# Weight sums for a seven-product last down projection, moved from the first FFN to the second up projection

## The chip, the cores and the metric

One core of a Trainium2 chip runs the whole program. The metric is the device time of one launch in microseconds (us). The engines are named as in the profile: PE (TensorE matmul), PEld (its weight load), DVE (VectorE), ACT (ScalarE), POOL (GpSimd), SP (SyncE). POOL, SP and ACT also issue DMAs.

## The reference

A decoder trunk of two layers on 512 tokens of width 1024, all in float32. Each layer has a token mixer and then a gated MLP (FFN); one RMSNorm ends it. What matters here is the FFN:

```python
D_FF, CONV_WIDTH, DEPTH = 2816, 3, 2
def conv_ffn(h, w_up, conv_w, conv_b, w_down):
    u = h @ w_up                       # (512, 1024) @ (1024, 5632)
    up = jnp.pad(u, ((0, 0), (CONV_WIDTH - 1, 0), (0, 0)))
    c = conv_b
    for j in range(CONV_WIDTH):
        c = c + conv_w[j] * up[:, j:j + S]
    gate, val = jnp.split(c, 2, axis=-1)
    return (jax.nn.silu(gate) * val) @ w_down      # (512, 2816) @ (2816, 1024)
...
for l in range(DEPTH):
    ...
    x = x + conv_ffn(rmsnorm(x, norm2_g[l]), ffn_w_up[l], ffn_conv_w[l], ffn_conv_b[l], ffn_w_down[l])
return rmsnorm(x, final_g)
```

## The kernel before, in words

**Matmuls.** Every float32 operand is split into a rounded high part and a low remainder, and a product is made of three matmuls (`mm3`, L153): high by low, high by high, low by high. The high part is a copy by ACT (L140 for weights, L149 for activations), the low part a subtraction by DVE (L141, L150).

**Weights.** `unit` (L95) hands out 128 x 512 pieces of weights by a plan that a first dry pass has noted. SP loads a piece into one of three buffers `wr` (L127), ACT and DVE split it into `sh`/`sl` or `wh`/`wl` (`part`, L131), up to `AHEAD` pieces before PE needs it (three in the FFN). A buffer is free for the next load once DVE has made the low part.

**The order of the work.** A tile scheduler orders each engine's instructions, by its own times for them; what is passed through `keep_in_program_order` keeps the order in which the program emits it. Each engine's list is executed in order, and an instruction that waits holds up what stands behind it on its engine.

**The up projection** (`ffn_up`, L1072) makes 22 pairs of output tiles, a gate tile and a value tile of 128 channels by 512 tokens. An output tile takes 24 matmuls. DVE then multiplies it by the row norm (`fu`, L1100), ACT makes the first tap of the convolution with the bias (`cv`, L1102), DVE adds two more taps (L1103, L1104); after both tiles of a pair ACT makes the silu and DVE the product (`fth`, L1109). In the second layer every other iteration up to the 16th also transposes a block of the residual through DRAM (`turned`, L226: a DVE transpose and five DMAs on POOL).

**The last down projection** (`last`, L1154) is not made as 8 products of blocks, but by a Strassen-like scheme with 7: the two halves of the tokens and neighbouring blocks of 128 channels are combined, in activations and in weights. `halves` (L1121) combines the activations of a pair of iterations on DVE: sums and differences of 256 columns each (L1130, L1131, L1132, L1134), of which some are split at once and some go to DRAM (`ab`, `s4`) by POOL. L1134 writes its difference into the tile `b`, whose old content POOL has just sent to DRAM (L1129). The combined weights are four tiles of 128 x 512 for each of the 11 groups of two blocks. `last` uses weight kinds 7, 5, 6, 4 of each group first (six matmuls for each, from `tsum`, DRAM tiles named `ts`), then the plain ones.

**The weight sums** (`presum`, L238). For each of the 11 groups POOL loads four tiles `pre` from `wdt` (L254), DVE makes four sums in place (L243 to L246, `b3 -= b1`, `b1 -= b0`, `b0 += b3`, `b2 -= b0`), and POOL stores them into `ts` (L249). This doesn't depend on any activation. A table, `PRE`, puts groups 0 to 3 at iterations 2, 4, 6 and 8 of the first layer's up projection, in 16 tiles of the FFN's large pool, and groups 4 to 10 at output tiles 0 to 6 of the first layer's down projection, in tiles of the general pool `u`; each call makes the sums of the group loaded by the call before. The scheduler is free to place them.

Of the kernel before, what the change touches and what calls it, by code (L numbers as in the profile page):

```python
# [15 lines left out]
L = 2  # L16
# [3 lines left out]
NFF = 22  # L20
# [3 lines left out]
FIRST = (12, 4, 0, 8)  # L24
FILL = (36, 2, 1)
KEPT = 6
PRE = {(0, "f", 2): 0, (0, "f", 4): 1, (0, "f", 6): 2, (0, "f", 8): 3, (0, "d", 0): 4, (0, "d", 1): 5, (0, "d", 2): 6, (0, "d", 3): 7,
       (0, "d", 4): 8, (0, "d", 5): 9, (0, "d", 6): 10}
SEQ = "0 H 0 S 0 U S U S 0 S 0 0 S 2 2 Y 0 0 2 1 2 1 2 1 2 1 2 1 2 1 1 1"
NRAW = 3  # L30
AHEAD = {None: 2, "p": 4, "r": 3, "f": 3, "u": 5, "q": 4}
DEEP = 6
EXP_HALF = math.exp(-0.5)
# [19 lines left out]
class Emit:  # L53
    def __init__(self, ctx, tc, a, plan=None):

        self.plan, self.used = plan, []
        self.raws, self.parts, self.nraw, self.npart = [], [], 0, 0
        self.pool, self.fp, self.pin, self.keep, self.turn = None, None, False, False, 4
        self.tc, self.nc, self.a = tc, tc.nc, a
        tp = lambda n, b, **k: ctx.enter_context(tc.tile_pool(name=n, bufs=b, **k))  # L60
        self.cp = tp("cp", 1)
        self.wp = tp("wp", 2)
        self.up = tp("up", NU)
        self.rg = tp("rg", NR)
        self.sp = tp("sp", 2)
        self.pa = tp("pa", 4, space=bass.MemoryType.PSUM)
        self.ps = tp("ps", 4, space=bass.MemoryType.PSUM)
        self.dp = tp("dp", 1, space=bass.MemoryType.DRAM)
        self.cnt = 0
# [52 lines left out]
    def load(self, u):  # L122
        name, l, i, c0, n, _ = u
        raw = self.u(n="wr") if u[5] == "q" and self.nraw % 2 else self.wp.tile([128, 512], F32, name=self.nm("wr"), tag="wr", bufs=NRAW)
        src = self.tsum[i] if name == "tsum" else self.a[name][l, i]
        with self.tc.high_priority():
            self.kept(self.nc.sync.dma_start(raw[:, :n], src[:, c0:c0 + n]))  # L127
        self.raws.append(raw)
        self.nraw += 1
# [105 lines left out]
        q.dma_start(d, t)  # L235
        return d

    def presum(self, l, stage, m):  # L238

        if self.pre:  # L240
            q, b = self.pre.pop()
            V = self.nc.vector
            V.tensor_tensor(b[3], b[3], b[1], op=SUB)  # L243
            V.tensor_tensor(b[1], b[1], b[0], op=SUB)
            V.tensor_tensor(b[0], b[0], b[3], op=ADD)
            V.tensor_tensor(b[2], b[2], b[0], op=SUB)  # L246
            for p, t in zip((7, 5, 6, 4), (b[3], b[1], b[0], b[2])):
                self.tsum[q, p] = self.dp.tile([128, 512], F32, name=self.nm("ts"))
                self.nc.gpsimd.dma_start(self.tsum[q, p], t)  # L249
        q = PRE.get((l, stage, m))  # L250
        if q is not None:
            b = self.fpre.pop(0) if stage == "f" else [self.u(n="pre") for _ in range(4)]
            for i, t in enumerate(b):
                self.nc.gpsimd.dma_start(t, self.a["wdt"][0, 2 * q + i // 2][:, i % 2 * 512:i % 2 * 512 + 512])  # L254
            self.pre.append((q, b))

    def norm_new(self):
        return {"z": [], "acc": None}
# [77 lines left out]
    def run(self):  # L336
        nc, tc, a, V = self.nc, self.tc, self.a, self.nc.vector
        self.con = self.cp.tile([128, NCC], F32, name="con")
        self.pre, self.tsum = [], {}
        self.rst = self.cp.tile([128, 512], F32, name="rst")  # L340
        self.bonesR = self.cp.tile([128, 128], F32R, name="bonesR")
        self.ones = self.cp.tile([128, 128], F32R, name="ones")
        V.memset(self.rst, 1.0)
        wu = self.acc()
        for i in range(5):
            nc.tensor.matmul(wu[:, 0:256], self.rst[:, 0:128], self.rst[:, 256:512], start=True, stop=True)
        self.pc = self.sp.tile([128, 64], F32, name="g1", tag="g1", bufs=1)
        st = self.norm_new()
        xs = [self.u(n="x") for _ in range(8)]
        self.keep = True  # L350
        with tc.high_priority():
            tc.keep_in_program_order(nc.scalar.dma_start(self.pc[:, 0:8], a["pcols"][0][:, PC["n1"]:PC["n1"] + 8]))
            for j in range(8):
                tc.keep_in_program_order((nc.scalar if j in (1, 3) else nc.sync).dma_start(xs[j], a["xT"][:, j, :]))
                if self.plan and j in (0, 1, 2):
                    self.load(self.plan[self.nraw])
        tc.keep_in_program_order(nc.scalar.copy(self.small((128, 1), "ms"), self.rst[:, 0:1]))
        tc.keep_in_program_order(nc.scalar.copy(self.ones, self.rst[:, 0:128]))
        for step in "z0 w z1 w z2 w z3 s0 s1 w z4 s2 z5 s3 w c z6 s4 w z7 s5 s6 s7 w w".split():
            if step == "w":  # L360
                if self.plan:
                    if self.nraw == self.npart:
                        self.load(self.plan[self.nraw])
                    self.part(self.plan[self.npart])
            elif step == "c":
                g1 = self.pc
                self.load_pc(0)
                tc.keep_in_program_order(nc.scalar.dma_start(self.con, a["con"]))
                self.pc, g1 = g1, self.pc
            elif step[0] == "z":  # L370
                self.norm_z(st, xs[int(step[1])], "n1")
            else:
                self.norm_sq(st, xs[int(step[1])])
        self.keep, self.pc = False, g1
        xd = [a["xT"][:, j, :] for j in range(8)]
        for l in range(L):
            mg = self.mixer(l, st)
            st = self.norm_new()
            x = self.wout(l, mg, xd, st)
            st["sq"] = self.split(st["acc"])  # L380
            act = self.ffn_up(l, st, x if l == L - 1 else None)
            if l == L - 1:
                self.last(act)
            else:
                st = self.norm_new()
                x, xd = self.ffn_down(l, act, x, st)
                st["sq"] = self.split(st["acc"])
            self.rp.__exit__(None, None, None)
            self.fp = None
# [682 lines left out]
    def ffn_up(self, l, st, x):  # L1072
# [7 lines left out]

        act, pair = [], []
        first = self.firstF(l, (78, 79, 80), st, 3)
        if l == 0:
            self.fpre = [[self.f(n="pre") for _ in range(4)] for _ in range(4)]
        for i in range(NFF):
            if l == 0 and i % 2 == 0 and 2 <= i <= 10:
                self.presum(l, "f", i)
            if x and i % 2 == 1 and i < 17:
                o = self.r(n="xt")
                self.turned(o, self.r(n="xT"), x[i // 2], nc.gpsimd)  # L1090
# [3 lines left out]
            for j in (i, NFF + i):  # L1094
                ps = first.pop(0) if first else self.colF(l, 78 + 2 * i + (j >= NFF))
                if pair:
                    act.append(self.halves(*pair, i // 2 - 1, at))
                    pair = []
                u = self.u(n="fu")
                V.tensor_tensor(u, ps, self.rsF, op=MUL)  # L1100
                t = self.u(n="cv")
                A.activation(t, u, AF.Identity, scale=self.p("cw2", j), bias=self.p("cb", j))  # L1102
                V.scalar_tensor_tensor(t[:, 1:], u[:, :511], self.p("cw1", j), t[:, 1:], op0=MUL, op1=ADD)  # L1103
                V.scalar_tensor_tensor(t[:, 2:], u[:, :510], self.p("cw0", j), t[:, 2:], op0=MUL, op1=ADD)  # L1104
                cs.append(t)
            g, v = cs
            th = self.u(n="fth")
            A.activation(th, g, AF.Silu)
# [12 lines left out]
    def halves(self, a, b, q, at):  # L1121
# [9 lines left out]
        V.tensor_tensor(s[:, h[1]], s[:, h[0]], a[:, h[0]], op=SUB)  # L1131
        V.tensor_tensor(d[:, h[0]], b[:, h[0]], s[:, h[1]], op=SUB)  # L1132
        P.dma_start(self.s4[:, h[q % 2]], d[:, h[0]])
        V.tensor_tensor(b[:, h[0]], a[:, h[0]], a[:, h[1]], op=SUB)  # L1134
        return self.split(s, at), self.split(b, at), ab, self.s4

    def ffn_down(self, l, act, x, st):
        nc, V = self.nc, self.nc.vector
# [2 lines left out]
        for m in range(8):  # L1141
# [5 lines left out]
            d = self.dp.tile([128, 512], F32, name=self.nm("xd"))  # L1147
            nc.gpsimd.dma_start(d, x[m])
            xd.append(d)
            self.presum(l, "d", m)  # L1150
        return x, xd


    def last(self, act):  # L1154
# [7 lines left out]

        def unit(p, q):
            if p > 3:
                return self.unit("tsum", 0, (q, p), 0)
            return self.unit("wdt", 0, 2 * q + (p > 1), 512 * (p == 3))

        def prod(ps, x, at, r, w, first, end, **kw):
# [27 lines left out]
        def half(ps):  # L1196
            t = self.u(n="e")
            po(A.activation(t, ps, AF.Copy, scale=0.5))
            return t
# [25 lines left out]
        for q in range(Q):  # L1225
            self.keep = q > 1
            s, t = act[q][:2]
            for p in (7, 5, 6, 4) if q < Q - 1 else (6, 7, 5, 4):
# [6 lines left out]
                if q == Q - 1 and p in (6, 7):  # L1235
                    for r in range(2):
                        (e1 if p == 6 else f0).append(half(pss[p][r]))
            if q == 1:
                for h in range(2):
                    nc.gpsimd.dma_start(fg[h], self.a["fgr"][:, H[h]].to_broadcast([128, 512]))  # L1240
# [216 lines left out]
```

## Time and profile before

| | us |
|---|---|
| median of 3 runs | 1702.33 (1700.75 to 1704.58) |
| the profiled execution's own time | 1699.76 |
| its span in the profile | 1697.8 |
| second up projection, 1000 matmuls in a row | 226.68 |

In a window's line of the profile there stand the stretch, its length, then for PE, PEld, DVE, ACT and POOL the busy time and in brackets the number of instructions, the clock granted to PE (1.00 is full), the share of time that the DMA engines are busy, and GB/s. In a line of a group, after the bar, stand the busy time in all, the mean of one in ns, another bar, the idle time of the engine just before these instructions and what ended it. In a line of waits stand the total, the number and the longest. In a line of the order of time stand the start and the length, in us. A line with "ns min/median/max" gives the length of one. In the last part of the page, a line of DMA issues ends with the size of one and the median us from issue to landing.

### The profile page before, as it was taken

How to read it: one execution, taken by the hardware profiler on the slowest of the kernel's cores; microseconds unless marked ns; L12 is line 12 of the kernel's file. 1: busy time of each engine (PE TensorE's matmuls, PEld its weight loads, DVE VectorE, ACT ScalarE, POOL GpSimd, SP SyncE). 2: the span in 40 equal slices, each digit the busy share in tenths (PEclk: the TensorE clock that was granted, in tenths of full speed). 3: DMA queues.
4: the chain of work that ended last, by engine and by line, in shares of the span. 5: the costliest groups of instructions: out<-in, count | busy, mean ns of one | idle time of the engine just before them, and what ended most of it. 6: DMA issues, size and time to landing. Idle time of an engine off the chain costs nothing.

```text
span 1697.8 us, 27852 instructions
## 1 busy us (share of the span) xinstructions
PE 1685.7 (99%) x10214; PEld 1379.7 (81%) x10214; DVE 1217.6 (72%) x2113; ACT 793.9 (47%) x1367; POOL 240.8 (14%) x336
## 2 busy tenths in 40 slices
PE   9999999999999999999999999999999999999998
PEld 7888777888888888888888887778888888888886
DVE  7887745578668877655568878455786698887776
ACT  6563443554255444433345634335542544444565
POOL 1121000003301200003321210000132012220000
PEclk9999999999999999999999999999999999999999
DMA  5236553624544532147743265535254534443775
GB/s 182 87 110 204 178 176 96 180 92 162 189 146 147 194 124 94 63 146 265 253 140 100 91 204 182 178 101 186 87 165 159 155 100 137 143 143 115 245 240 169
DMA packets 147768, 260.01 MB, mean 153 GB/s; under 512 B 19600, under 2 KB 39952, under 8 KB 147632
## 3 DMA queue, kind: packets, MB, share of 16 engines
q1 hardware_dynamic: 122960, 192.87, 36.1%
q0 software_dynamic: 15888, 49.95, 8.9%
q10 hardware_dynamic: 8784, 15.42, 2.6%
q8 instruction: 80, 1.31, 0.3%
q14 instruction: 56, 0.46, 0.1%
HBM read 212.94 MB, written 45.22 MB: 152 GB/s over the span
## 4 chain that ended last, share of the span: by engine, by line
PE 88%; DVE 5%; DMA 3%; ACT 1%; issue 1%; SPq 0%; ACTq 0%; DVEq 0%
PE acc L157 80%; PE sm L157 3%; PE sm L678 2%; DMA wr<-wall 2%; DVE wl L141 1%; PE sm L931 1%; PE sm L585 1%; DVE cs L804 1%; DVE TMP L802 1%; ACT wh L140 1%; DMA tr<-bkT 0%; DVE sl L141 0%; PE sm L1036 0%; DMA bkS<-tr 0%; ACT sh L140 0%
## 5 line engine op out<-in xcount | busy, mean ns | idle before, releaser
L157 PE MATMUL acc<-hi,sh 128*128 128x512 f32 x1108 | 431.9, 390 | 0.0
L157 PE MATMUL acc<-lo,sh 128*128 128x512 f32 x1108 | 431.6, 390 | 0.0
L157 PE MATMUL acc<-hi,sl 128*128 128x512 f32 x1108 | 424.5, 390 | 0.0
L140 ACT CAST sh<-wr 128x512 fp32r<-128x512 f32 (+1 forms) x375 | 226.6, 614 | 299.0 <-PE acc L157 153.1
L141 DVE TENSOR_TENSOR sl<-wr,sh 128x512 fp32r<-128x512 f32 (+1 forms) x375 | 253.7, 684 | 104.6 <-ACT sh L140 80.3
L141 DVE TENSOR_TENSOR wl<-wr,wh 128x512 fp32r<-128x512 f32 x238 | 169.3, 714 | 145.3 <-ACT wh L140 140.0
L140 ACT CAST wh<-wr 128x512 fp32r<-128x512 f32 x238 | 146.8, 619 | 243.4 <-PE acc L157 139.6
L157 PEld LDWEIGHTS acc<-lo,sh 128*128 128x128 f32 x1108 | 208.0, 188 | 44.0 <-issue 0.9
L157 PEld LDWEIGHTS acc<-hi,sl 128*128 128x128 f32 x1108 | 207.9, 188 | 43.6 <-DVE gth L1051 0.3
L157 PEld LDWEIGHTS acc<-hi,sh 128*128 128x128 f32 x1108 | 208.0, 188 | 43.1 <-issue 0.3
L157 PE MATMUL acc<-lo,wh 128*128 128x512 f32 x588 | 231.8, 394 | 0.0
L157 PE MATMUL acc<-hi,wl 128*128 128x512 f32 x588 | 230.1, 391 | 1.2 <-DVE wl L141 1.2
L157 PE MATMUL acc<-hi,wh 128*128 128x512 f32 x588 | 229.3, 390 | 0.0
L1102 ACT ACTIVATE cv<-fu,pc 128x512 f32<-128x512 f32 x88 | 71.7, 816 | 139.3 <-DVE fu L1100 139.3
L157 PEld LDWEIGHTS acc<-hi,wl 128*128 128x128 f32 x588 | 110.3, 188 | 26.6 <-DVE wl L141 2.8
L157 PEld LDWEIGHTS acc<-lo,wh 128*128 128x128 f32 x588 | 110.4, 188 | 24.5 <-ACT wh L140 0.6
L157 PEld LDWEIGHTS acc<-hi,wh 128*128 128x128 f32 x588 | 110.4, 188 | 22.4 <-issue 0.2
L157 PE MATMUL acc<-ah,sh 128*128 128x512 f32 x352 | 108.4, 389 | 0.0
L1103 DVE SCALAR_TENSOR_TENSOR cv<-fu,pc,cv 128x511 f32<-128x511 f32 x88 | 65.9, 750 | 34.5 <-ACT cv L1102 34.5
L157 PE MATMUL acc<-wl,hi 128*128 128x512 f32 x212 | 86.1, 406 | 0.0
L1100 DVE TENSOR_TENSOR fu<-acc,rsF 128x512 f32<-128x512 f32 x88 | 60.4, 686 | 31.7 <-PE acc L157 30.8
L157 PE MATMUL acc<-wh,lo 128*128 128x512 f32 x212 | 82.8, 390 | 0.0
(358 smaller groups left out, 2415.2 us busy)
## 6 DMA issues: line engine op xcount, KB each, us to landing
wr<-wall SPq DMA_DIRECT2D x480, 256.0 KB, 2.9
gd<-gth ACTq DMA_DIRECT2D x48, 256.0 KB, 3.2
gth<-gd POOLq DMA_DIRECT2D x48, 256.0 KB, 3.7
pre<-wdt POOLq DMA_DIRECT2D x44, 256.0 KB, 5.9
ts<-pre POOLq DMA_DIRECT2D x44, 256.0 KB, 2.8
wr<-ts SPq DMA_DIRECT2D x44, 256.0 KB, 4.0
wr<-wdn SPq DMA_DIRECT2D x40, 256.0 KB, 3.9
wr<-wdt SPq DMA_DIRECT2D x33, 256.0 KB, 3.6
```

What stands on the lines that cost most here:

```text
L140: self.kept(self.nc.scalar.copy(hi[:, :n], raw[:, :n]))
L141: self.kept(self.nc.vector.tensor_tensor(lo[:, :n], raw[:, :n], hi[:, :n], op=SUB))
L157: i = self.nc.tensor.matmul(*x, **y, **kw)
L585: i = T.matmul(pK[hv[1 - h], j, :], bk[hv[h], c, 1, :], x[hv[h], c, :], start=True, stop=True)
L678: po(T.matmul(o, l, r, start=start, stop=True, skip_group_check=True))
L802: V.tensor_tensor(tmp, NS[:, k + 1:, k:k + 1].to_broadcast([128, r, c]), TS[:, k:k + 1, :c].to_broadcast([128, r, c]), op=MUL)
L804: V.tensor_tensor(TS[:, k + 1:, :c], TS[:, k + 1:, :c], tmp, op=ADD)
L931: po(T.matmul(X[h][:, i, :], lhsT, rhs, start=new[h], stop=stop, skip_group_check=True))
L1100: V.tensor_tensor(u, ps, self.rsF, op=MUL)
L1102: A.activation(t, u, AF.Identity, scale=self.p("cw2", j), bias=self.p("cb", j))
L1103: V.scalar_tensor_tensor(t[:, 1:], u[:, :511], self.p("cw1", j), t[:, 1:], op0=MUL, op1=ADD)
```

## The change

The 11 groups of sums move from the first layer's FFN to the second layer's, written as a generator that is advanced by calls. The first call comes ahead of the loop of the up projection; then one after the second tile of each even iteration and one after each tile of an odd one, up to iteration 19; the last two come after groups 1 and 2 of `last`. Of each three calls, the first issues a group's four loads, the second and the third make two sums each and issue their stores. All are kept in program order. Their tiles are six of their own (a pool `pp`), and the ring for the descriptors of POOL's DMAs is set to 4096 bytes of a partition in place of the default. In `halves` the difference that L1134 wrote into `b` goes to the free half of the tile `wl` instead, and its high and low parts are made in two halves of 256 columns.

```diff
-PRE = {(0, "f", 2): 0, (0, "f", 4): 1, (0, "f", 6): 2, (0, "f", 8): 3, (0, "d", 0): 4, (0, "d", 1): 5, (0, "d", 2): 6, (0, "d", 3): 7,
-       (0, "d", 4): 8, (0, "d", 5): 9, (0, "d", 6): 10}
+RING = 4096
...
+        self.pp = tp("pp", 6)
...
-    def presum(self, l, stage, m):
...
+    def sums(self, l):
+        P, V, po = self.nc.gpsimd, self.nc.vector, self.tc.keep_in_program_order
+        for q in range(NFF // 2):
+            b = [self.pp.tile([128, 512], F32, name=self.nm("pre"), tag="pre") for _ in range(4)]
             for i, t in enumerate(b):
+                po(P.dma_start(t, self.a["wdt"][l - 1, 2 * q + i // 2][:, i % 2 * 512:i % 2 * 512 + 512]))
+            yield
+            for p, o, x, op in ((7, 3, 1, SUB), (5, 1, 0, SUB), (6, 0, 3, ADD), (4, 2, 0, SUB)):
+                po(V.tensor_tensor(b[o], b[o], b[x], op=op))
+                self.tsum[l, q, p] = self.dp.tile([128, 512], F32, name=self.nm("ts"))
+                po(P.dma_start(self.tsum[l, q, p], b[o]))
+                if p == 5:
+                    yield
+            yield
+
+    def presum(self, l, ok=True):
+        if ok and l == L - 1:
+            next(self.sum, None)
...
     def ffn_up(self, l, st, x):
-        if l == 0:
-            self.fpre = [[self.f(n="pre") for _ in range(4)] for _ in range(4)]
+        self.sum = self.sums(l)
+        self.presum(l)
         for i in range(NFF):
-            if l == 0 and i % 2 == 0 and 2 <= i <= 10:
-                self.presum(l, "f", i)
...
                 cs.append(t)
+                self.presum(l, i < NFF - 2 and (i % 2 or j > i))
...
     def halves(self, a, b, q, at):
-        V.tensor_tensor(b[:, h[0]], a[:, h[0]], a[:, h[1]], op=SUB)
-        return self.split(s, at), self.split(b, at), ab, self.s4
+        V.tensor_tensor(d[:, h[1]], a[:, h[0]], a[:, h[1]], op=SUB)
+        t = hi, lo = at(), at()
+        for o, x in ((h[0], d[:, h[1]]), (h[1], b[:, h[1]])):
+            self.nc.scalar.copy(hi[:, o], x)
+            V.tensor_tensor(lo[:, o], x, hi[:, o], op=SUB)
+        return self.split(s, at), t, ab, self.s4
...
     def ffn_down(self, l, act, x, st):
-            self.presum(l, "d", m)
...
     def last(self, act):
+            if 0 < q < 3:
+                self.presum(L - 1)
...
-        nc = _bacc.Bacc("TRN2", target_bir_lowering=False, num_devices=1)
+        nc = _bacc.Bacc("TRN2", target_bir_lowering=False, num_devices=1, dynamic_dma_scratch_size=RING)
```

More of the change, by code (lines that the diff above doesn't have):

```diff
@@ L124, in load @@
         raw = self.u(n="wr") if u[5] == "q" and self.nraw % 2 else self.wp.tile([128, 512], F32, name=self.nm("wr"), tag="wr", bufs=NRAW)
-        src = self.tsum[i] if name == "tsum" else self.a[name][l, i]
+        src = self.tsum[(l, *i)] if name == "tsum" else self.a[name][l, i]
         with self.tc.high_priority():
@@ L236, in trip @@
         return d
-    def presum(self, l, stage, m):
[L240 to L252, printed above, removed]
-            for i, t in enumerate(b):
-                self.nc.gpsimd.dma_start(t, self.a["wdt"][0, 2 * q + i // 2][:, i % 2 * 512:i % 2 * 512 + 512])
-            self.pre.append((q, b))
+    def sums(self, l):
+        P, V, po = self.nc.gpsimd, self.nc.vector, self.tc.keep_in_program_order
+        for q in range(NFF // 2):
+            b = [self.pp.tile([128, 512], F32, name=self.nm("pre"), tag="pre") for _ in range(4)]
+            for i, t in enumerate(b):
+                po(P.dma_start(t, self.a["wdt"][l - 1, 2 * q + i // 2][:, i % 2 * 512:i % 2 * 512 + 512]))
[10 more added lines that the diff above has]
+            next(self.sum, None)
     def norm_new(self):
@@ L338, in run @@
         self.con = self.cp.tile([128, NCC], F32, name="con")
-        self.pre, self.tsum = [], {}
+        self.tsum = {}
         self.rst = self.cp.tile([128, 512], F32, name="rst")
@@ L1164, in unit @@
             if p > 3:
-                return self.unit("tsum", 0, (q, p), 0)
+                return self.unit("tsum", L - 1, (q, p), 0)
             return self.unit("wdt", 0, 2 * q + (p > 1), 512 * (p == 3))
```

## The prediction

> **What bounds the kernel now.** I read the page first, then the waits of PE, then stretches of the span as windows, then VectorE's groups and waits inside the second up projection, and last the order of time around that stage's end. The page:
>
> ```profile
> span 1697.8 us, 27852 instructions
> PE 1685.7 (99%) x10214; PEld 1379.7 (81%) x10214; DVE 1217.6 (72%) x2113; ACT 793.9 (47%) x1367; POOL 240.8 (14%) x336
> ```
>
> TensorE (PE) is busy for all but 12.1 us. The windows (length, then busy time and count of PE, PEld, DVE, ACT, POOL, the clock, the DMA share, GB/s) say where those are not. In order: first up projection while it makes sums, the first down projection, the second up projection, the last 50 us:
>
> ```profile
> 513.80:600.00 86.20, 86.20 (x382) 71.37 (x381) 75.07 (x119) 44.39 (x68) 13.96 (x26) 1.00 0.53 176
> 750.00:855.00 105.00, 105.00 (x465) 86.93 (x464) 57.25 (x90) 32.33 (x56) 33.07 (x62) 1.00 0.76 251
> 1373.00:1579.00 206.00, 206.00 (x910) 170.57 (x910) 171.97 (x279) 92.19 (x154) 35.52 (x65) 1.00 0.43 136
> 1650.00:1700.00 50.00, 40.10 (x175) 32.44 (x174) 34.28 (x63) 24.28 (x52) 2.18 (x4) 0.96 0.50 164
> ```
>
> All three stages that the change touches run PE without a gap. The idle time lies in the last window (its span ends at 1697.8, so 47.8 - 40.1 = 7.7 us) and in places that are left as they are. So almost nothing can be won; the question is what VectorE (DVE) can carry more before PE waits for it. PE's pace, from the chain of waits, and one round of the second up projection (two iterations, four output tiles):
>
> ```profile
> 1357.13 226.68 PE acc L157 x1000
> 1362.27:1384.03 21.76, 21.76 (x98) 18.02 (x97) 19.95 (x33) 12.04 (x18) 3.68 (x7) 1.00 0.24 82
> 1481.96:1503.73 21.77, 21.77 (x98) 18.03 (x97) 18.18 (x29) 9.60 (x17) 4.39 (x8) 1.00 0.48 136
> ```
>
> A matmul takes 0.2267 us, an output tile (8 blocks of 128 rows, 3 matmuls each) 24 of them, 5.44 us, and a round 21.76 us. In that, DVE is busy 18.18 us and free 3.6.
>
> **The change part by part.** The result of the instruction order of the changed program, taken beside this one's: PE's list is the same throughout, SyncE's but for one place, and all else outside the two FFN stages and the last projection is the same. So only these stages can move.
>
> *Removed from the first FFN:* 16 sums in its up projection, 28 in its down projection, 44 loads and 44 stores on POOL. PE has 86.20 of 86.20 and 105.00 of 105.00 there: worth 0. Nothing is late next, as nothing was late.
>
> *Added to the second up projection:* 40 of the 44 sums, four per round for ten rounds, and their DMAs; none in its last two iterations. The remaining four come after groups 1 and 2 of the last projection. What a sum costs, what a neighbour costs back to back, and what DVE waits for in one round:
>
> ```profile
> L243 DVE TENSOR_TENSOR pre<-pre,pre x4: 685/687/689, 536.4 to 596.2; 128x512 f32<-128x512 f32 x4
> 1392.39 1.29 DVE L141 TENSOR_TENSOR sl<-wr,sh 128x512 fp32r<-128x512 f32 x2
> L141 DVE TENSOR_TENSOR sl<-wr,sh 128x512 fp32r<-128x512 f32 x8 | 5.4, 686 | 0.9 <-ACT sh L140 0.9
> L1103 DVE SCALAR_TENSOR_TENSOR cv<-fu,pc,cv 128x511 f32<-128x511 f32 x4 | 3.0, 750 | 2.0 <-ACT cv L1102 2.0
> L150 DVE TENSOR_TENSOR ah<-fth,ah 128x512 fp32r<-128x512 f32 x1 | 0.7, 687 | 0.0
> L1134 DVE TENSOR_TENSOR fth<-fth 128x256 f32<-128x256 f32 x1 | 0.4, 426 | 0.0
> DVE cv L1103 <- ACT cv L1102: 21.3, 29, 0.9
> ```
>
> A sum is 0.687 us long, but two neighbours take 1.29 us together, so one in a queue costs 0.60. Four make 2.4 to 2.75 us a round. The halved split (one operation of 0.687 becomes two of 0.426) adds up to 0.165. So the round is 18.18 + 2.4 = 20.6 at least, 18.18 + 2.75 + 0.165 = 21.1 at most. To it come waits for ScalarE: 0.9 us each time `cv` follows `fu` with nothing between, 21.3 us over the stage. In the old order 25 of 44 pairs stand bare, in the new one 11, about one per round: the sums sit in that gap. With one such wait the round is 21.5 to 22.0 against PE's 21.76: between 0.26 spare and 0.24 over. Ten rounds over make 2.4 us of lateness at worst; split weights are made up to three units of 12 matmuls (2.72 us each) ahead, and the last two iterations have no sums, so this lateness is covered. If the cover is gone it costs up to 2.4. I take 0.
>
> *The stage's first round* is tighter: DVE is at 19.95 of 21.76 there (it comes out of the norm), and the order puts six sums beside it, 3.6 us: 23.55, so 1.8 us late. Two units of lead (5.4) would cover it, none would not: 0 to 1.8, I take 0.7, as the units here are made just after the norm and are few.
>
> *The ScalarE part* (a copy of 512 columns becomes two of 256): ScalarE is busy 9.60 of 21.77, so 0; its bare price would be one instruction's overhead, below the 0.165 above.
>
> *The start of the last projection.* Here PE does lose time now:
>
> ```profile
> 1592.76 0.61 PE L157 MATMUL sm<-wh,ah 128*128 128x512 f32 x2
> 1593.39 0.50 PE L157 MATMUL sm<-wl,ah 128*128 128x512 f32 x1
> 1593.73 0.64 PE L157 MATMUL sm<-wh,ah 128*128 128x512 f32 x2
> ...
> 1595.83 0.62 PE L157 MATMUL acc<-sh,ah 128*128 128x512 f32 x2
> 1596.71 0.50 PE L157 MATMUL acc<-sl,ah 128*128 128x512 f32 x1 [0.26 <-DVE sl L141]
> 1597.04 0.62 PE L157 MATMUL acc<-sh,ah 128*128 128x512 f32 x2
> ```
>
> At 0.2267 each, the starts at 1593.39, 1593.73, 1596.71 and 1597.04 are late by 0.18, 0.11, 0.43 and 0.10: 0.8 us. One cause goes: DVE's write into the tile that a POOL DMA still reads.
>
> ```profile
> 1592.31 0.43 DVE L1134 TENSOR_TENSOR fth<-fth 128x256 f32<-128x256 f32 x1 [0.90 <-DMA ab<-fth]
> 1596.00:1602.00 6.00, 5.74 (x25) 4.43 (x25) 4.52 (x8) 2.95 (x6) 0.00 (x0) 1.00 1.00 357
> 1602.00:1608.00 6.00, 6.00 (x28) 4.95 (x28) 4.49 (x8) 4.41 (x9) 0.00 (x0) 1.00 1.01 347
> ```
>
> Writing the difference to another tile takes that 0.90 away from DVE, so up to 0.8 of PE's time may come back. Late next are the weight splits, for the same stretch gets four sums (2.4 us of DVE; it is busy 4.5 of each 6 us, so about 1.5 of 6 are free) and four stores of 0.26 MB where the DMA engines are already full (share 1.00 at 357 GB/s): 1.05 MB is 2.9 us of them. Bounds: -0.8 (the wait goes, the rest is hidden) and +2.9 (loads late by the whole transfer). I take +0.5, nearer to the low end, as the row at 1602 shows PE at 6.00 of 6.00 with the engines full: some weight tiles are there ahead.
>
> *POOL and its queue.* The issues, and the landings (the page, us at the line's end):
>
> ```profile
> L249 POOL DMA_DIRECT2D ts<-pre x16: 539/542/547, 537.3 to 601.5; - x16
> L254 POOL DMA_DIRECT2D pre<-wdt x12: 536/541/543, 543.4 to 581.9; - x12
> ...
> L231 POOL DMA_DIRECT2D xt<-tr x4 | 2.2, 556 | 2.8 <-issue 2.8
> ...
> wr<-wall SPq DMA_DIRECT2D x480, 256.0 KB, 2.9
> pre<-wdt POOLq DMA_DIRECT2D x44, 256.0 KB, 5.9
> ts<-pre POOLq DMA_DIRECT2D x44, 256.0 KB, 2.8
> wr<-wdn SPq DMA_DIRECT2D x40, 256.0 KB, 3.9
> ```
>
> Per round POOL issues 4 loads, 4 stores, and the 8 of now: 16 x 0.55 = 8.8 of 21.76 us. With six tiles the third and fourth load of a group wait for stores of the group before (2.8 us), and the transposes' and halves' DMAs queue behind them; nobody on PE's path waits for those. A load lands 5.9 us after its issue and its sums stand two tiles (10.9 us) later. Cost 0; uncovered, DVE would wait the 5.9 per group. The same density was run already: four groups between 513.80 and 600.00, DVE at 75.07 of 86.20, and PE lost nothing. The smaller descriptor ring (4096 in place of the default) I cost at 0 too; no row shows a POOL issue waiting for room, and its price, if it bites, is rival D's.
>
> A rule of the Trainium skill speaks against the change: "SBUF — State Buffer", section "SBUF: two separate sides", says that a DMA issued by GpSimd needs descriptors that GpSimd cannot write while VectorE holds the shared port in a 2-port mode, and warns of fp32 copies. By its figures (about 620 ns alone, 3100 beside a copy) 16 issues would need some 40 us more a round, an estimate from that page. The rows above speak against it: 28 issues beside such sums and splits took 536 to 547 ns, none longer.
>
> **Sum.** 0 + 0.7 + 0.5 = +1.2 us. The profiled execution itself took 1699.76 (span 1697.8 and 1.96 around it), 2.57 below the median of 1702.33. On it the sum gives 1700.96; on the median, 1703.5, which I predict.
>
> **The rivals.**
> A, slower: DVE becomes the bound of the stage. If weight loads land at 3.9 us as beside the first down projection (DMA share 0.76) instead of 2.9, the wait for a cast (0.9 a round now) comes once more: 22.0 + 0.9 = 22.9, 1.14 over per round, 11.4 in ten. Beyond two units of lead (5.4) PE waits 6.0: 1708.3. It decides from 21.76 + 0.54 per round on. For it: the ledger is within 0.3 us of full and DMA traffic grows. Against: the first up projection, at the same density, lost nothing (but at 87% of DVE, here 95 to 97).
> B, slower: the four late stores hit the full DMA engines: the upper bound 2.9 with 0.7 and, as the sums push the splits too, 0.5: 1706.4. For it: share 1.00. Against: PE was fed there.
> C, a little faster: only the removed wait counts: 1702.33 - 0.8 = 1701.5. PE has no further gap in these stages, so a gain of 0.2% (3.4 us, about what a measurement of this kernel can tell from no change) isn't to be had.
> D, slower: POOL is held, by ring or port. If each of 16 issues also waits out one DVE operation, 16 x (0.55 + 0.69) = 19.8, with the two landings of 2.8 in its chain 25.4 a round, 3.6 over, 36 in ten: 1738.
> That the change would not do what it says is excluded by the order: the sums stand in the second up projection.
>
> **How the numbers follow.** The forecast (0 to +3.4, centre 1703.5) 0.67, A 0.13, B 0.10, C 0.07, D 0.03. Slower by over 0.2%: 0.13 + 0.10 + 0.03 = 0.26; faster by over 0.2%: 0.02 out of C, should a run fall low; same 0.72. The range takes in C with a microsecond of scatter and A: 1700.5 to 1709.0, leaving out D and little else.
>
> **What would show it.** Right: PE without a gap from 1373 to 1579 but for under 1 us near the fourth to eighth tile; DVE busy about 21 of 21.76 a round; `pre` waiting for no DMA; the 0.90 at L1134 gone. Wrong: PE waiting for `sl` in round after round (A), ScalarE's casts waiting longer for `wr<-ts` between 1594 and 1612 (B), POOL issues over 0.6 us or waits of `pre` for its load (D), or PE's count of matmuls per window above the old one.

## The result and the profile after

| | us |
|---|---|
| before, median of 4 runs | 1701.78 (1700.75 to 1704.58) |
| changed, median of 4 runs | 1719.44 (1718.33 to 1721.46) |
| ratio, 95% interval | 1.0106 [1.0094, 1.0117] |

The change makes the kernel 17.7 us slower. The forecast was no change (1703.5, at most 1709.0).

First, where the time lies. Two marks cut the span: the last matmul of the row norm ahead of the second up projection (its last start is the end of the line), and the first matmul of the last projection (the first start). Before:

```profile
L283 PE MATMUL sm<-hi,ones x3: 389/389/389, 508.7 to 1356.7; 128*128 128x512 f32 x3
L157 PE MATMUL acc<-wl,ah x28: 389/389/400, 1583.6 to 1642.4; 128*128 128x512 f32 x28
```

The changed kernel, whose line numbers differ by one (L284 here is L283 before; in the up projection L1102 is L1103 before):

```profile
L284 PE MATMUL sm<-hi,ones x3: 389/389/389, 511.3 to 1360.6; 128*128 128x512 f32 x3
L157 PE MATMUL acc<-wl,ah x28: 389/389/504, 1602.5 to 1663.3; 128*128 128x512 f32 x28
```

The second up projection grew from 226.9 us (1356.7 to 1583.6) to 241.9, by 15.0. From there to the end of the span it is 114.2 before and 115.8 after (the changed span is 1718.3), 1.6 more. The 3.9 us ahead of it I take for scatter: the experiments below, whose code is the same in the stages of most of that time, reach this mark between 1354.4 and 1360.9 in their profiles, the fastest and the slowest of them with the sums where the changed kernel has them.

The changed kernel's page, and a window in the middle of the stage:

```profile
span 1718.3 us, 27811 instructions
...
PE 1693.5 (99%) x10214; PEld 1377.6 (80%) x10214; DVE 1212.3 (71%) x2124; ACT 799.3 (47%) x1378; POOL 241.2 (14%) x336
...
PE 75%; DVE 9%; DMA 8%; issue 3%; ACT 2%; SPq 1%; POOL 0%; ACTq 0%; DVEq 0%
```

```profile
1400.00:1550.00 150.00, 144.14 (x618) 114.38 (x617) 125.77 (x216) 63.05 (x108) 53.20 (x99) 1.00 0.67 221
```

The same window before:

```profile
1400.00:1550.00 150.00, 150.00 (x663) 124.20 (x663) 123.78 (x199) 67.02 (x112) 27.94 (x51) 1.00 0.44 137
```

The page before has, for the last of these lines:

```profile
PE 88%; DVE 5%; DMA 3%; ACT 1%; issue 1%; SPq 0%; ACTq 0%; DVEq 0%
```

It gives the chain that ended last by engine: PE's share fell from 88% to 75%, DVE's grew from 5% to 9% and DMA's from 3% to 8%. In the window there are 618 matmuls where there were 663, so 45 x 0.2267 = 10.2 us of 150 are lost (PE's busy time, whose ends are modelled, shows only 5.9 of it). What PE's weight loads wait for is VectorE's low part `sl`, here from 1345 us to the end, changed and before:

```profile
PEld acc L157 <- DVE sl L141: 14.6, 16, 1.5
```

```profile
PEld acc L157 <- DVE sl L141: 1.6, 2, 0.9
```

The first surprise is DVE: it has 40 sums more in this stage, and it is busy hardly longer, 125.77 of 150. It isn't full; it stands still. What DVE, then ACT waits for in the changed kernel from 1357 to 1600 (total, times, longest), and how long a load into `wr` takes to land from 1380 to 1580:

```profile
DVE sl L141 <- ACT sh L140: 23.0, 23, 2.2
DVE cv L1102 <- ACT cv L1101: 8.2, 10, 0.9
```

```profile
ACT sh L140 <- DMA wr<-wall: 63.2, 33, 5.9
```

```profile
DMA to landing us min/median/max: 2.5/3.8/7.6
```

The waits for casts and for loads, and the landings, before:

```profile
DVE sl L141 <- ACT sh L140: 2.7, 4, 0.9
```

```profile
ACT sh L140 <- DMA wr<-wall: 10.4, 7, 2.6
```

```profile
DMA to landing us min/median/max: 2.5/2.9/4.3
```

ScalarE's cast of a weight piece waits for the load, 63.2 us instead of 10.4, and VectorE's low part waits for the cast, 23.0 instead of 2.7. (The `cv` line is VectorE's wait for the first tap, which now has sums beside it.) The median landing went from 2.9 to 3.8, the longest from 4.3 to 7.6. One such load stands in nearly every round. An example, in the chain of the changed kernel:

```profile
1494.95 0.69 DVE sl L141
1495.66 6.32 DMA wr<-wall
1502.09 0.63 ACT sh L140
1503.35 0.70 DVE xT L228
```

and POOL's order of time just ahead of it:

```profile
1492.41 2.13 POOL L244 DMA_DIRECT2D pre<-wdt  x4
```

A buffer comes free when `sl` has been made from it, at 1495.64; the load into it starts at 1495.66, one microsecond after POOL has issued a row of four loads of `pre` (1492.41 to 1494.54), and takes 6.32 us; the cast follows, and the next `sl` from this buffer can start at 1502.74. From `sl` to `sl` that is 7.79 us. Three buffers at PE's pace have 3 x 2.72 = 8.16 us. So 0.4 us are left for all other waiting of DVE and ACT in that turn, and what they lose, the next load starts late by. Lines like the second, 5.6 to 6.6 us long, come in nine of the ten rounds of the chain.

### The profile page after: what moved, and what is told of

Its sections match the earlier page's. It is cut to its first block, busy times and chain, and to the rows that moved or that the text cites. A ratio compares the mean times of both kernels' runs of the same rounds, so it can differ in the third digit from the quotient of the medians.

```text
span 1718.3 us, 27811 instructions
## 1 busy us (share of the span) xinstructions
PE 1693.5 (99%) x10214; PEld 1377.6 (80%) x10214; DVE 1212.3 (71%) x2124; ACT 799.3 (47%) x1378; POOL 241.2 (14%) x336
## 4 chain that ended last, share of the span: by engine, by line
PE 75%; DVE 9%; DMA 8%; issue 3%; ACT 2%; SPq 1%; POOL 0%; ACTq 0%; DVEq 0%
PE acc L157 67%; DMA wr<-wall 5%; PE sm L157 3%; PE sm L679 2%; DVE sl L141 2%; DVE wl L141 1%; DVE cv L1102 1%; DVE pre L247 1%; PE sm L932 1%; DVE cv L1103 1%; ACT sh L140 1%; DVE fu L1099 1%; PE sm L586 1%; DMA tr<-qkt 1%; DMA xt<-tr 0%
## 5 line engine op out<-in xcount | busy, mean ns | idle before, releaser
L157 PE MATMUL acc<-wh,hi 128*128 128x512 f32 x212 | 82.8, 390 | 0.0
L1102 DVE SCALAR_TENSOR_TENSOR cv<-fu,pc,cv 128x511 f32<-128x511 f32 x88 | 65.6, 747 | 24.1 <-ACT cv L1101 24.1
```

The source lines that it names most:

```text
L157: i = self.nc.tensor.matmul(*x, **y, **kw)
```

## The experiments

Times are compared with the kernel before, run beside each: it took 1701.28 us beside the first four experiments, 1698.05 beside the next four, 1702.13 beside the last two. The windows of 1400 to 1550 us lie in the second up projection of each.

**Transfers and sums apart.** First, the loads and stores with hardly any of VectorE's work, each sum cut to 8 of its 512 columns:

```diff
-                po(V.tensor_tensor(b[o], b[o], b[x], op=op))
+                po(V.tensor_tensor(b[o][:, 0:8], b[o][:, 0:8], b[x][:, 0:8], op=op))
```

> The changed kernel with each of the 44 sums cut to 8 of its 512 columns (the other columns of the combined weights are left unsummed); its loads, stores and their places stay. In the changed kernel's profile the second up projection takes 15.0 us longer than before (241.9 against 226.9), and in each round one weight load lands 6.3 us after its issue, just behind the four loads of a group. Theory T, late landings and a full VectorE together: VectorE gets back about 2.2 us a round, so most of the 15 goes: 1703 to 1707 us. Rival M, the DMAs alone: the late landings stay and so does the time, 1715 to 1720. Rival V, VectorE's work alone: 1701 to 1704, and the landings don't matter. Rival N, the small descriptor ring: 1719.

Measured: 1703.18 us, ratio 1.0015 [1.0005, 1.0025]; the stage takes 227.9 us (before 226.9). Its window and the landings of weight loads:

```profile
1400.00:1550.00 150.00, 149.54 (x659) 123.19 (x659) 124.46 (x231) 68.44 (x118) 57.22 (x106) 1.00 0.68 226
```

```profile
DMA to landing us min/median/max: 2.5/4.2/8.8
```

The landings are as long as in the changed kernel, even longer (median 4.2, longest 8.8), and PE loses next to nothing. Rival M is out: late landings alone don't cost the time. The longest, 8.8 us, is alone over the 8.16 that the turn of the buffers has, and PE makes 659 matmuls here, four fewer than before.

Then the sums without the transfers:

```diff
-            b = [self.pp.tile([128, 512], F32, name=self.nm("pre"), tag="pre") for _ in range(4)]
-            for i, t in enumerate(b):
-                po(P.dma_start(t, ...))
+            if q == 0:
+                b = [self.pp.tile([128, 512], F32, name=self.nm("pre"), tag="pre") for _ in range(4)]
+                for i, t in enumerate(b):
+                    po(P.dma_start(t, ...))
...
-                self.tsum[l, q, p] = self.dp.tile([128, 512], F32, name=self.nm("ts"))
-                po(P.dma_start(self.tsum[l, q, p], b[o]))
+                if q:
+                    self.tsum[l, q, p] = self.tsum[l, 0, p]
+                else:
+                    self.tsum[l, q, p] = self.dp.tile([128, 512], F32, name=self.nm("ts"))
+                    po(P.dma_start(self.tsum[l, q, p], b[o]))
```

> The changed kernel with the 44 sums in their places but loads and stores of the first group only (all groups sum the same four tiles again and the last projection reads the first group's sums for all). Theory T: without the loads, weight loads land at 2.9 us again and VectorE, though full, keeps up: 1702 to 1706 us. Rival M: 1701 to 1704. Rival V: the sums alone cost the time, 1715 to 1720, with VectorE busy over 95% of the second up projection. Rival N: 1719 if the ring itself slows, since the ring is as small.

Measured: 1703.78 us, ratio 1.0017 [1.0007, 1.0027]. Its window:

```profile
1400.00:1550.00 150.00, 150.00 (x664) 124.20 (x663) 136.70 (x235) 68.37 (x117) 27.55 (x50) 1.00 0.44 136
```

All sums in their fixed places, and PE runs 150.00 of 150 with 664 matmuls. Rival V is out too. DVE is busy 136.70 of 150, which is 91%, not over 95. Apart, each half costs some 2 us; together 17.7. Theory T stands in that it takes both; its full VectorE does not show.

**The ring, and the new `halves`.** In the kernel before, one edit each time:

```diff
-        nc = _bacc.Bacc("TRN2", target_bir_lowering=False, num_devices=1)
+        nc = _bacc.Bacc("TRN2", target_bir_lowering=False, num_devices=1, dynamic_dma_scratch_size=4096)
```

> The kernel before with nothing changed but the descriptor ring of POOL's DMAs set to 4096 bytes. Theory T and rivals M and V: no change, within 2 us of 1702. Rival N: slower, by the 2.6 us that the changed kernel's profile is late by the time of the first FFN's norm (511.3 against 508.7, in code that is the same) up to the whole 18.

Measured: 1701.56 us, 1.0007 [0.9998, 1.0016]; the stage is 226.9 us. Rival N is out. The second (the change's edit to `halves`, in the kernel before):

> The kernel before with only the new form of halves: the difference goes to the free half of another tile, its split is made in two halves. The prediction's term: -0.8 to 0 us, since the 0.90 us wait at L1134 goes (1701 to 1702). Rival H, that the new form holds up the weight splits on ScalarE, where the casts of 256 columns stand in order ahead of weight casts: 1704 or more.

Measured: 1701.21 us, 0.9999 [0.9990, 1.0009]. The wait at L1134 is gone. A wait for ScalarE's cast of a weight piece stays; the first line below is from the kernel before, which had this wait besides the other, the second from the kernel with the new `halves`:

```profile
1594.76 0.69 DVE L141 TENSOR_TENSOR wl<-wr,wh 128x512 fp32r<-128x512 f32 x1 [0.82 <-ACT wh L140]
```

```profile
1594.22 0.69 DVE L141 TENSOR_TENSOR wl<-wr,wh 128x512 fp32r<-128x512 f32 x1 [0.69 <-ACT wh L140]
```

From the first matmul of the last projection to the end its profile takes 114.2 us, as before. The edit is worth nothing that can be told from no change, and rival H is out.

**Which transfers.** Three kernels to see whether the row of four loads, the bytes, or one kind of transfer is at fault. One spreads them, with a sum, its store and one load of the next group behind each tile:

```diff
...
+        b, free = {i: fetch(0, i, t[k]) for k, i in enumerate((3, 1, 0, 2))}, t[4:]
+        yield
+        for q in range(NFF // 2):
+            new = {}
+            for p, o, x, op, n in ((7, 3, 1, SUB, 3), (5, 1, 0, SUB, 1), (6, 0, 3, ADD, 0), (4, 2, 0, SUB, 2)):
+                po(V.tensor_tensor(b[o], b[o], b[x], op=op))
...
+                po(P.dma_start(self.tsum[l, q, p], b[o]))
+                if q < NFF // 2 - 1:
+                    new[n] = fetch(q + 1, n, {3: free[0], 1: free[1], 0: b[1], 2: b[3]}[n])
+                yield
+            b, free = new, [b[0], b[2]]
```

> The changed kernel with the same 44 sums, loads and stores, spread evenly: one sum, one store and one load for the next group after each output tile from the second to the 41st, in the same six tiles. Theory T2: VectorE's list has no room for a late weight load, and the one late load per round (6.3 us) comes from four loads issued in a row. Without the row weight loads land below 5 us: 1702 to 1707 us, the second up projection under 231 us. Rival B, the bytes and not the row: 8 transfers a round delay the weight loads however they are spread: 1712 to 1720. Rival W, a sum behind each tile is a worse place than two behind some: over 1707 though no landing exceeds 5 us.

Measured: 1702.71 us against 1698.05 beside it, ratio 1.0028 [1.0016, 1.0039]; the stage takes 230.3 us. Its window, the landings of weight loads, and VectorE's wait for casts:

```profile
1400.00:1550.00 150.00, 148.87 (x654) 122.04 (x653) 133.84 (x230) 66.98 (x115) 57.62 (x107) 1.00 0.70 228
```

```profile
DMA to landing us min/median/max: 2.6/3.8/6.8
```

```profile
DVE sl L141 <- ACT sh L140: 8.9, 10, 1.7
```

Three quarters of the loss go with the same bytes and the same sums, so the order in time of the sums and transfers matters. But the landings did not come below 5 us as expected: the median is 3.8 as in the changed kernel, the longest 6.8. So "without the row no late load" was wrong. Rivals B and W, both slower than this, are out.

The other two leave out one kind of transfer after the first group, the stores or the loads (by the edits shown above):

> The changed kernel with all loads and sums, but the stores of the first group only (the last projection reads the first group's sums for all). Theory T2: the row of four loads is what matters, so most of the time stays: 1711 to 1718 us, one weight load per round landing above 5.5 us. Rival B: half the bytes, half the loss, 1706 to 1711.

Measured: 1701.83 us, 1.0021 [1.0012, 1.0031]; the stage takes 229.9 us. The window and the landings:

```profile
1400.00:1550.00 150.00, 150.00 (x663) 124.25 (x662) 136.67 (x235) 69.58 (x119) 43.13 (x79) 1.00 0.56 185
```

```profile
DMA to landing us min/median/max: 2.3/3.0/6.2
```

> The changed kernel with all sums and stores, but the loads of the first group only (all groups sum the same four tiles again). Theory T2: stores come one or two at a time, weight loads land below 5 us: 1702 to 1706 us. Rival B: 1706 to 1711.

Measured: 1699.45 us, 1.0008 [0.9999, 1.0017]; the stage takes 227.8 us.

With all sums and the rows of four loads, PE keeps 150.00 of 150 in this window. So the row of loads is not the cause by itself, and this part of theory T2 falls: 1711 to 1718 was expected. The 3.0 us that this kernel's stage does lose lie ahead of the window, in a round that still has the first group's stores beside the second group's loads, as in the changed kernel (shown further down). The bytes don't add up either (1.0021 and 1.0008 against 1.0106). With the loads alone the median landing is 3.0 (6.2 at most), with the stores alone 3.1 (4.4 at most), and the window is full; with both it is 3.8, and PE loses matmuls there.

**The buffers.** If what breaks is the turn of the three buffers, a fourth must mend it, with sums, transfers and landings as they are:

```diff
-NRAW = 3
-RING = 4096
+NRAW = 4
+RING = 2048
```

> The changed kernel with four buffers wr for raw weights in place of three; the descriptor ring shrinks to 2048 bytes to make room. A load can then start one piece (2.72 us) sooner. Theory T2: the late load is absorbed, the casts wait less, the second up projection takes 227 to 232 us and the whole 1702 to 1708. Rival V2, that the sums' fixed places in VectorE's order cost the time: the landings stay as long and the time too, 1714 to 1720. If the smaller ring holds POOL up, its issues get longer than 0.57 us.

Measured: 1698.04 us, ratio 1.0001 [0.9992, 1.0011]. The window, the wait for casts and the landings:

```profile
1400.00:1550.00 150.00, 150.00 (x664) 124.24 (x663) 137.03 (x234) 68.49 (x118) 58.21 (x107) 1.00 0.68 231
```

```profile
DVE sl L141 <- ACT sh L140: 1.0, 3, 0.5
```

```profile
DMA to landing us min/median/max: 2.6/3.8/7.3
```

The landings are those of the changed kernel (3.8, 7.3 at most), VectorE is busy 137.03 of 150, and in the window nothing is lost; its waits for casts fell from 23.0 to 1.0 us. The stage takes 229.1 us (1354.4 to 1583.5): of the 15.0 us lost, 12.8 are back, and the other 2.2 lie in its first two rounds (shown further down). That the whole time comes out equal is also due to the last projection, which takes 112.7 us from its first matmul to the end where the kernel before takes 114.2.

So after the first rounds the loss needs three things at once: the transfers, the sums and only three buffers (and, as the kernel that spreads them shows, an order in time in which they meet). The first experiment had longer landings and the second as busy a VectorE, and neither lost it; here both are there and a fourth buffer takes it away. They meet in the turn of a weight buffer: load, cast, low part, and the next load waiting for that low part. Rival V2 is out, and the ring of 2048 does no harm that shows: POOL's issues take 538 to 568 ns.

**Controls, and a version that beats both.** A fourth buffer might help anywhere, so the kernel before got it too, as shown; a second kernel has NRAW = 6 and the new `halves`:

```diff
-NRAW = 3
+NRAW = 4
...
+        nc = _bacc.Bacc("TRN2", target_bir_lowering=False, num_devices=1, dynamic_dma_scratch_size=4096)
```

> The kernel before with four buffers wr in place of three (descriptor ring 4096), nothing else: the control for the changed kernel with four buffers, which took 1.0001 of the time before. Theory T3: the buffer mends only what the change broke, so the old kernel gains nothing from it, within 1.5 us of before. Rival G, that a fourth buffer is worth 2 to 4 us anywhere (that run reached the second up projection 2.3 us sooner than before's profile): 0.9975 to 0.9988, and then the change with four buffers still costs 2 to 4 us against its own control.

> The kernel before with six buffers wr and the new form of halves: the version that would beat both, if anything here does. Theory T3: TensorE idles 12 us, of which at most 1 us is for weights, so 0.999 to 1.000. Rival G: 0.997 to 0.9985.

Measured: 0.9987 [0.9978, 0.9997] with four, 1699.53 us against 1702.13; 0.9969 [0.9958, 0.9980] with six and the new `halves`, 1697.72 us. So rival G was nearer: a fourth buffer is worth 2 to 3 us to the kernel before, of which 1.6 show in its profile from the last projection on (112.6 us against 114.2). The changed kernel with four still stands about 0.14% behind its own control, though their intervals overlap at 0.9992 to 0.9997; the control's stage is as long as before, 226.9 us, so these 0.14% fit the 2.2 us that the changed one lost in its first rounds. The kernel before with six buffers is the fastest that was run; how much of its gain is the buffers' alone wasn't tried, but `halves` alone gave 0.9999, and its profile doesn't show where the gain lies.

## Why the prediction was wrong

*The first FFN, worth 0.* Right. With the sums gone the changed kernel's PE has what it had:

```profile
500.00:550.00 50.00, 50.00 (x222) 41.42 (x221) 41.29 (x63) 27.98 (x43) 0.00 (x0) 1.00 0.35 106
750.00:800.00 50.00, 50.00 (x222) 41.42 (x221) 19.88 (x31) 16.94 (x29) 1.63 (x3) 1.00 0.41 120
```

*VectorE's round, 20.6 to 21.1 us busy and at most 22.0 with one wait, cost 0.* For the sums alone right in its result, and on the high side: they make 136.70 / 150 x 21.76 = 19.8 busy, and PE lost nothing in that window.

*The stage's first round, +0.7 (0 to 1.8).* Right for the sums alone, too low with the loads beside them. With the sums, and transfers of the first group only, the stage is 0.9 us longer (227.8 against 226.9); with the loads of all groups as well 3.0; with everything and four buffers 2.2. With four buffers, PE was idle 0.64 and 1.01 in the first two rounds:

```profile
1354.00:1376.00 22.00, 21.36 (x95) 17.36 (x94) 19.43 (x31) 9.88 (x15) 5.36 (x10) 1.00 0.27 86
1376.00:1398.00 22.00, 20.99 (x93) 17.06 (x92) 20.52 (x37) 9.97 (x17) 8.75 (x17) 1.00 0.82 268
```

The second of these windows in the kernel before, in the changed kernel and in the one with loads and sums:

```profile
1376.00:1398.00 22.00, 22.00 (x99) 18.21 (x97) 19.68 (x34) 11.35 (x19) 4.93 (x9) 1.00 0.47 155
```

```profile
1376.00:1398.00 22.00, 19.80 (x85) 15.43 (x84) 19.72 (x36) 9.93 (x18) 9.79 (x19) 1.00 0.64 211
```

```profile
1376.00:1398.00 22.00, 19.84 (x86) 15.43 (x85) 19.76 (x35) 9.56 (x17) 9.54 (x18) 1.00 0.65 219
```

The changed kernel makes 14 matmuls fewer than the kernel before, 3.2 of its 15.0 us. The kernel with loads and sums loses nearly as many: it too has the first group's stores and the second group's loads in this round, and only later no stores. The step counted the sums of this round and no transfers.

*The start of the last projection, +0.5 (-0.8 to 2.9).* Within its bounds, at 1.6 us. Of the -0.8 nothing showed: with `halves` alone the stretch stayed at 114.2 us, though the interval of the times would not exclude 0.8.

*POOL and its queue, "Cost 0".* Here it failed. The step priced the 16 issues on POOL, the landing of the sums' own loads and the waits of POOL, and all of that held well enough: those loads landed in 6.8 us in the median (5.9 was priced), and the new issues took

```profile
L249 POOL DMA_DIRECT2D ts<-pre x40: 539/539/566, 1371.0 to 1583.8; - x40
L244 POOL DMA_DIRECT2D pre<-wdt x40: 536/541/550, 1379.3 to 1585.9; - x40
```

and no sum waited for its load. (The Trainium skill, in "SBUF — State Buffer", section "SBUF: two separate sides", says that POOL can't write its descriptors while VectorE runs in a 2-port mode, which an fp32 copy within SBUF triggers. The sums aren't copies, and 80 issues beside them, of 536 to 566 ns, show no hold.) What the step left out is what these transfers do to SP's: "nobody on PE's path waits for those" looked at who waits for POOL's DMAs, and not at who shares the DMA engines with them. That stood only in rival A, at 0.13, and A had the landing right (3.9 forecast, 3.8 measured) but priced it as one more wait of 0.9 a round, 6.0 us in all. It came to 23 waits, 23.0 us, and 15.0 us of PE. A also took VectorE for the bound of the stage, but it was busy 125.77 of 150 and waited. The turn of the buffers was missing from the step and from A: a late load makes a late `sl`, and the next load into that buffer waits for that `sl`. So, as I read it, lateness comes back instead of being paid once.

*"The same density was run already."* True, and misleading. The first up projection with its sums has 33 weight loads; their landings, and what ACT and DVE waited for ahead of casts and low parts there:

```profile
DMA to landing us min/median/max: 2.5/2.7/5.8
```

```profile
  PE acc L157: 31.5, 27
  ACT sh L140: 0.7, 1
```

They waited for PE and for no load: the pieces were made as far ahead as they may be. In the second up projection, before the change, the same list begins with the load:

```profile
  DMA wr<-wall: 9.5, 6
  ACT sh L140: 2.7, 4
```

and has no wait for PE. There VectorE also combines activations and transposes, and the turn of the buffers was short of slack already. That row was to be had before the prediction.

What stays open: the ledger of one turn, 7.79 us of 8.16 at 1494.95, is from one round, and how the lateness spreads from buffer to buffer over a round is argued from it, not shown. The loads' own landing doesn't decide it: with transfers alone they landed later, 4.2 us in the median, and PE kept its pace. What delays the first rounds was not taken apart. Also why the first FFN's loads hardly delay the weight loads there (2.7 us) and the same loads do here (3.0 to 3.8) wasn't tried; the transposes' and the halves' transfers share the engines only in the second.

## What to carry to other kernels

Two additions that are each hidden may not be hidden together: here 1.0015 for the transfers, 1.0017 for the vector work, 1.0106 for both, and a fourth buffer took most of it away, because both draw on the same slack, the turn of a few load buffers. So price that turn (landing, cast, low part, and every wait between them in the engines' order) against buffers times PE's pace, not only each engine's busy time. When an engine gets more work and isn't busier, look for what it stands still for; one more buffer may be the cheapest cure, and is a good test of the cause.

## What was not expected of the hardware

The descriptor ring of POOL's DMAs could shrink to 4096 bytes at 1.0007 [0.9998, 1.0016], and to 2048 with POOL issues of 538 to 568 ns, as long as the others. With the ring at 4096 and six weight buffers in place of three (and the new `halves`, worth nothing alone) the old kernel gained 0.3%, though its page shows PE busy for 1685.7 of 1697.8 us before.
